# Ranking the weight split and the emptying of PSUM tiles sixty instructions earlier in a two-layer decoder trunk

## The chip, the cores and the metric

One core of one Trainium2 chip runs the whole kernel. The metric is the device time of one execution in microseconds (us); the time before is the median of three runs, 2280.33 us (2279.54 to 2280.35).

## The reference, cut to what matters

Two residual layers act on 256 tokens of width 2048, in float32. Each layer projects a normalised input to three groups of attention heads, mixes them back with `w_o`, and then runs a gated MLP with a short convolution:

```python
h = _rmsnorm(x, attn_norm[l])
z = jnp.einsum('bsd,de->bse', h, w_in[l])
...
x = x + jnp.einsum('bsm,md->bsd', mix, w_o[l])
h = _rmsnorm(x, ffn_norm[l])
u = jnp.einsum('bsd,df->bsf', h, w_up)          # 2048 -> 2 * 5632
u = conv(u) + conv_b                            # causal, 3 taps, per channel
a, g = jnp.split(u, 2, axis=-1)
x = x + jnp.einsum('bsf,fd->bsd', jax.nn.silu(g) * a, w_down)
```

All weights are float32, 410 MB in total, and each is used once.

## The kernel before, in words

**Weights.** The weights come as one stream of 128x128 blocks. `load` (L108) brings a chunk of 16 blocks (1 MB) into one of three `raw` tiles through the queue of SP. `convert` (L127) splits a piece of 8 blocks into two fp32r parts: ACT casts `raw` to `hi` (L139) and DVE subtracts to get `lo` (L140). There are five `hi` and five `lo` tiles, so a new piece can be cast only after TensorE (PE) has used up the piece five before it. `weights` (L145) hands a block out; at the first block of a piece it converts the piece two ahead (L150) and loads the next two chunks (L151, L152).

**Matmuls.** `mm_t` (L181) makes one 128-column output tile of all 256 tokens in a PSUM tile `mm`: 16 matmuls with `hi` against 512 columns (L193, both parts of the activations side by side) and 16 with `lo` against 256 columns (L198). It needs two pieces. Calls alternate: one does all of its `hi` first and then `lo`, the next does one `hi`, then `lo`, then the other fifteen `hi`. `mm_v` (L235) makes output tiles with tokens on the partitions (L247 to L249). `total` (L254) empties an `mm` tile of `mm_t`: ACT copies the second half out (L256), DVE adds the first half to it (L258).

**The MLP's up projection.** In each half of each layer, 22 pairs of tiles are made, an `a` tile and then a `g` tile. Of each tile, after `total`: GpSimd (POOL) multiplies by the norm's scale (L821), ACT applies a tap and the bias (L824), DVE adds two taps (L825, L826). After the second tile of a pair follow silu on ACT (L828), the product on POOL (L829), and the split of the result on ACT and DVE (L507, L508 in `to_hl`). After the 22 pairs, `residual` (L453) multiplies with `w_down` by `mm_v` and DVE adds the result to `x` (L458).

**What sets the order.** Every engine runs its instructions in the order in which they stand in its queue. That order is made by the framework's planner when the kernel is built. Each instruction has a rank, its place in the program. The planner keeps a clock of its own with an estimated duration for each instruction; whenever an engine is free on that clock, it gives it, among the instructions whose inputs are finished and whose tiles can be had, the one with the lowest rank. So an instruction that the program writes later often stands earlier in a queue, because it could run earlier on the planner's clock. On the chip the queue's order is then fixed, whatever the real durations are. `tc.high_priority(offset=60)` lowers the rank of the instructions in its block by 60, and these instructions do not advance the count of ranks. In one pair of the up projection the program has 90 instructions (64 matmuls, 8 of `convert`, 2 loads, 4 of `total`, 12 others).

Of the kernel before, what the change touches and what calls it, by code (L numbers as in the profile page):

```python
# [13 lines left out]
ALU = mybir.AluOpType  # L14
# [3 lines left out]
T = 256  # L18
# [8 lines left out]
MAGIC = 12582912.0  # L27
CH = 16
SUB = 8

C_ID, C_MASK, C_INVF, C_SIGN, C_EPS, C_SEL, C_ONE = 0, 128, 384, 386, 388, 390, 396
C_W = C_ONE + P
# [34 lines left out]
def kernel(ctx: ExitStack, tc: tile.TileContext, xin, xnat, pos, wstream, cst, par, fin, out):  # L67
    nc = tc.nc
# [10 lines left out]
    def nm(s):  # L79
        uid[0] += 1  # L80
        return f"{s}_{uid[0]}"
# [4 lines left out]
    def tmp():  # L86
        return work.tile([P, T], F32, tag="tmp", name=nm("tmp"), bufs=15)
# [10 lines left out]
    def f(ap):  # L98
        return ap.bitcast(F32)
# [4 lines left out]
    raws, subs = {}, {}  # L104
    bounds = [(c, i, min(SUB, n - i)) for c, (at, n) in enumerate(chunks) for i in range(0, n, SUB)]
    sub_of = {chunks[c][0] + o + i: (s, i) for s, (c, o, n) in enumerate(bounds) for i in range(n)}

    def load(c):  # L108
        if c >= nch or c in raws:
            return  # L110
        at, n = chunks[c]
        t = wpool.tile([P, CH * P], F32, tag="raw", name=nm("raw"), bufs=3)
        nc.sync.dma_start(t[:, : n * P], wflat[at * P * P : (at + n) * P * P].rearrange("(p e) -> p e", p=P))
        raws[c] = t
# [12 lines left out]
    def convert(s, between=None):  # L127
        if s >= len(bounds) or s in subs:
            return
        c, o, n = bounds[s]  # L130
        load(c)
        o = o * P
        src = raws[c][:, o : o + n * P]
        hi = wpool.tile([P, SUB * P], F32R, tag="hi", name=nm("hi"), bufs=5)
        lo = wpool.tile([P, SUB * P], F32R, tag="lo", name=nm("lo"), bufs=5)
        step = SUB // 2 * P if c < 3 else SUB * P
        for o in range(0, n * P, step):
            a = slice(o, min(o + step, n * P))
            nc.scalar.copy(hi[:, a], src[:, a])  # L139
            nc.vector.tensor_tensor(lo[:, a], src[:, a], f(hi[:, a]), ALU.subtract)  # L140
            if between is not None:
                between()
        subs[s] = (hi, lo)

    def weights(b, n=1):  # L145
        s, o = sub_of[b]
        if o == 0:
            convert(s)
            convert(s + 1)
            convert(s + 2)  # L150
            load(bounds[s][0] + 1)  # L151
            load(bounds[s][0] + 2)  # L152
        o *= P
        hi, lo = subs[s]
        return hi[:, o : o + n * P], lo[:, o : o + n * P]
# [25 lines left out]
    def mm_t(moving):  # L181
        ps = bank("mm", 3)
        k = len(moving)
        ws = []
        for i in range(k):
            ws.append(weights(cb[0]))
            cb[0] += 1
        flip = turn_of[0] % 2
        turn_of[0] += 1

        def high(part):
            for i in part:
                nc.tensor.matmul(ps, ws[i][0], moving[i], start=(i == 0), stop=bool(flip and i == k - 1))  # L193

        n = 1 if flip else k
        high(range(n))
        for i in range(k):
            nc.tensor.matmul(ps[:, :T], ws[i][1], moving[i][:, :T], start=False, stop=(not flip and i == k - 1))  # L198
        high(range(n, k))
        return ps  # L200

    def mm_first(moving, hooks={}, tag="mm", bufs=3):
        ps = bank(tag, bufs)
        k = len(moving)
        for i, mv in enumerate(moving):
            if i in hooks:
                hooks[i]()
            hi, lo = weights(cb[0])
            cb[0] += 1
            if i < k - 1:  # L210
                nc.tensor.matmul(ps, hi, mv, start=(i == 0), stop=False)
                nc.tensor.matmul(ps[:, :T], lo, mv[:, :T], start=False, stop=False)
            else:
                nc.tensor.matmul(ps[:, :T], lo, mv[:, :T], start=(i == 0), stop=False)
                nc.tensor.matmul(ps, hi, mv, start=False, stop=True)
        return ps

    def mm_t2(moving, hooks={}):
        ps = [bank("mm", 3) for _ in range(2)]
        k = len(moving)  # L220
        for i, mv in enumerate(moving):
            if i in hooks:
                hooks[i]()
            hi, lo = weights(cb[0], 2)
            cb[0] += 2
            for j in range(2):
                a = slice(j * P, (j + 1) * P)
                if i == 0:
                    nc.tensor.matmul(ps[j], hi[:, a], mv, start=True, stop=False)
                nc.tensor.matmul(ps[j][:, :T], lo[:, a], mv[:, :T], start=False, stop=False)  # L230
                if i:
                    nc.tensor.matmul(ps[j], hi[:, a], mv, start=False, stop=(i == k - 1))  # L232
        return ps
# [18 lines left out]
        return ps  # L252

    def total(ps, rows=P):  # L254
        t = tmp()
        nc.scalar.copy(t[:rows], ps[:rows, T : 2 * T])  # L256
        u = tmp()
        nc.vector.tensor_tensor(u[:rows], ps[:rows, :T], t[:rows], ALU.add)  # L258
        return u

    pr = [const.tile([P, Q_W], F32, tag=f"par{l}", name=f"par{l}") for l in range(DEPTH)]
# [301 lines left out]
    for l in range(DEPTH):  # L563
# [11 lines left out]
        else:  # L575
            first = mm_t2(hx, {4: lambda: norm.turn(3), KT // 2: norm.cols})
        rstd = norm.rows("rstd")
        u = total(first[0], 70)
        kf = tmp()
        nc.vector.tensor_tensor(kf[:70], u[:70], rstd[:70], ALU.mult)  # L580
# [23 lines left out]
        for i in range(8):  # L604
            a, b = scan[i % 2], scan[(i + 1) % 2]
            s = 1 << i
# [33 lines left out]
        for j in range(2):  # L640
            for h in range(H_FOX):
                if j == 0:
                    fqk.append(slot())
                i = j * H_FOX + h + 1
                u = total(first[i] if i < len(first) else mm_t(hx))
                nc.gpsimd.tensor_tensor(fqk[h][:, j * T : (j + 1) * T], u, rstd if j else rstd_f, ALU.mult)
                tick()
# [32 lines left out]
        for j in range(2):  # L680
            for h in range(H_DIFF):
                if j == 0:
                    aqk.append(slot())
                u = total(mm_t(hx))
                nc.gpsimd.tensor_tensor(aqk[h][:, j * T : (j + 1) * T], u, rstd if j else rstd_a, ALU.mult)
                if j == 1:
                    bg.append(rope_job(aqk[h][:], slot()[:], 0))
                tick()
# [43 lines left out]
        for qo in (Q_KN, Q_QN):  # L732
            ln = Norm(q_[:, qo : qo + 4], 512)
            tiles = []
            for k in range(4):
                u = total(mm_t(hx))
# [71 lines left out]
        for half in range(2):  # L808
            acts = []
            for i in range(HALF):  # L810
# [7 lines left out]
                for j in range(2):  # L818
                    u = total(pair[j] if pair else mm_t(hx))
# [181 lines left out]
```

## Time and profile before

| | |
|---|---|
| median of three runs | 2280.33 us |
| the profiled execution | 2280.38 us |
| its span, first to last instruction | 2278.2 us |
| busy: PE / DVE / ACT / POOL | 99% / 64% / 53% / 19% |
| granted PE clock, mean | 0.998 |
| DMA engines, mean busy share | about 0.5, 182 GB/s |

The profiled execution took 2.2 us more than its span, and agrees with the median to 0.05 us. The names of tiles in the rows are the program's: `hi`, `lo` and `raw` of the weights, `mm` for the PSUM tiles, `tmp` for the tiles of the steps after `total`.

### The profile page before, as it was taken

The numbers are of one execution on the slowest core, as the hardware profiler recorded it, in microseconds if no ns is written. First come the engines' busy times: TensorE is split into PE (matmuls) and PEld (weight loads), VectorE is DVE, ScalarE is ACT, GpSimd is POOL, SyncE is SP. The second block draws the span as 40 slices with busy tenths as digits, with TensorE's granted clock in tenths as the row PEclk, the third lists the DMA queues.
The fourth block names the chain that finished last, engine by engine and source line by source line (L and its number), as shares of the span: only waits on it lengthen the run. The fifth ranks groups of instructions, "written<-read, shape, count | busy, mean of one in ns | idle before, by whom it ended". The sixth has DMA issues, their size and how long they took to land.

```text
span 2278.2 us, 31040 instructions
## 1 busy us (share of the span) xinstructions
PE 2244.7 (99%) x12083; PEld 1931.5 (85%) x12083; DVE 1468.5 (64%) x2317; ACT 1198.6 (53%) x1867; POOL 436.6 (19%) x395
## 2 busy tenths in 40 slices
PE   9999999999999999999999999999999999999998
PEld 8888978888878888888888989788888888888886
DVE  8767766666664566665575677666666645777653
ACT  7456645555543455555454566456555434555543
POOL 4600000222210022220022001003333101222210
PEclk9999999999999999999999999999999999999999
DMA  8544344555555555545555444354555555555553
GB/s 314 203 149 167 142 149 176 173 179 169 182 197 191 185 178 173 184 168 204 189 181 201 150 165 153 138 183 178 185 185 186 208 197 185 187 191 193 205 198 116
DMA packets 60915, 413.59 MB, mean 182 GB/s; under 512 B 6880, under 2 KB 7008, under 8 KB 11744
## 3 DMA queue, kind: packets, MB, share of 16 engines
q1 hardware_dynamic: 60048, 410.54, 51.0%
q8 instruction: 95, 1.56, 0.3%
q10 hardware_dynamic: 720, 1.07, 0.1%
q14 instruction: 52, 0.43, 0.1%
HBM read 409.49 MB, written 2.10 MB: 181 GB/s over the span
## 4 chain that ended last, share of the span: by engine, by line
PE 84%; DVE 6%; ACT 5%; issue 3%; POOL 2%; DMA 0%; SPq 0%; ACTq 0%; POOLq 0%; DVEq 0%
PE mm L193 27%; PE mm L198 15%; PE mm L247 12%; PE mm L249 11%; PE mm L248 11%; DVE lo L140 4%; ACT hi L139 3%; PE s L470 2%; POOL tmp L821 2%; ACT tmp L824 1%; PE mm L232 1%; DVE tmp L825 1%; DVE tmp L826 1%; ACT tmp L828 1%; PE mm L763 1%
## 5 line engine op out<-in xcount | busy, mean ns | idle before, releaser
L140 DVE TENSOR_TENSOR lo<-raw,hi 128x1024 fp32r<-128x1024 f32 (+1 forms) x776 | 952.3, 1236 | 496.4 <-ACT hi L139 457.0
L139 ACT CAST hi<-raw 128x1024 fp32r<-128x1024 f32 (+1 forms) x776 | 799.3, 1039 | 469.1 <-PE mm L249 364.4
L193 PE MATMUL mm<-h,hi 128*128 128x512 f32 x3584 | 862.8, 392 | 0.0
L193 PEld LDWEIGHTS mm<-h,hi 128*128 128x128 f32 x3584 | 664.8, 188 | 134.5 <-ACT tmp L256 1.3
L198 PEld LDWEIGHTS mm<-h,lo 128*128 128x128 f32 x3584 | 462.0, 190 | 35.3 <-DVE lo L140 21.7
L198 PE MATMUL mm<-h,lo 128*128 128x256 f32 x3584 | 472.7, 284 | 15.8 <-DVE lo L140 15.8
L821 POOL TENSOR_TENSOR tmp<-tmp,rstd 128x256 f32<-128x256 f32 x176 | 224.3, 1274 | 1041.7 <-DVE tmp L258 731.7
L247 PE MATMUL mm<-hi,slot 128*128 128x512 f32 x992 | 388.8, 392 | 3.5 <-DVE tmp L258 3.5
L249 PE MATMUL mm<-hi,slot 128*128 128x512 f32 x992 | 385.5, 389 | 0.0
L248 PE MATMUL mm<-lo,slot 128*128 128x512 f32 x992 | 385.3, 388 | 0.0
L824 ACT ACTIVATE tmp<-tmp,par 128x256 f32<-128x256 f32 x176 | 105.9, 602 | 357.3 <-POOL tmp L821 357.1
L247 PEld LDWEIGHTS mm<-hi,slot 128*128 128x128 f32 x992 | 186.6, 188 | 46.1 <-DVE tmp L258 4.4
L249 PEld LDWEIGHTS mm<-hi,slot 128*128 128x128 f32 x992 | 186.6, 188 | 38.5
L248 PEld LDWEIGHTS mm<-lo,slot 128*128 128x128 f32 x992 | 186.8, 188 | 36.9
L825 DVE SCALAR_TENSOR_TENSOR tmp<-tmp,par,tmp 128x255 f32<-128x255 f32 x176 | 84.9, 482 | 204.0 <-ACT tmp L824 204.0
L829 POOL TENSOR_TENSOR tmp<-tmp,tmp 128x256 f32<-128x256 f32 x88 | 76.0, 863 | 208.8 <-ACT tmp L828 208.8
L256 ACT COPY tmp<-mm 128x256 f32<-128x256 f32 (+1 forms) x233 | 85.3, 366 | 56.5 <-PE mm L193 33.6
L258 DVE TENSOR_TENSOR tmp<-mm,tmp 128x256 f32<-128x256 f32 (+1 forms) x233 | 97.3, 417 | 4.3 <-ACT tmp L256 4.1
L826 DVE SCALAR_TENSOR_TENSOR tmp<-tmp,par,tmp 128x254 f32<-128x254 f32 x176 | 85.0, 483 | 6.2
L828 ACT ACTIVATE tmp<-tmp 128x256 f32<-128x256 f32 x88 | 36.8, 418 | 61.5 <-DVE tmp L826 61.4
L247 PE MATMUL mm<-hi,h 128*128 128x512 f32 (+1 forms) x192 | 68.3, 356 | 0.0
L249 PE MATMUL mm<-hi,h 128*128 128x512 f32 (+1 forms) x192 | 67.9, 354 | 0.0
(192 smaller groups left out, 1469.1 us busy)
## 6 DMA issues: line engine op xcount, KB each, us to landing
raw<-in_w SPq DMA_DIRECT2D x381, 1024.0 KB, 4.8
raw<-in_w SPq DMA_DIRECT2D x14, 256.0 KB, 5.4
slot<-in_x SPq DMA_DIRECT2D x8, 256.0 KB, 5.4
x<-in_xn SPq DMA_DIRECT2D x2, 1024.0 KB, 10.5
slot<-in_fin SPq DMA_DIRECT2D x4, 256.0 KB, 6.5
out<-x SPq DMA_DIRECT2D x4, 256.0 KB, 3.9
out<-x ACTq DMA_DIRECT2D x4, 256.0 KB, 4.2
par<-in_par SPq DMA_DIRECT2D x1, 325.0 KB, 7.5
```

The source lines that it names most:

```text
L139: nc.scalar.copy(hi[:, a], src[:, a])
L140: nc.vector.tensor_tensor(lo[:, a], src[:, a], f(hi[:, a]), ALU.subtract)
L193: nc.tensor.matmul(ps, ws[i][0], moving[i], start=(i == 0), stop=bool(flip and i == k - 1))
L198: nc.tensor.matmul(ps[:, :T], ws[i][1], moving[i][:, :T], start=False, stop=(not flip and i == k - 1))
L247: nc.tensor.matmul(ps[t][:, :n], s_hi, hi, start=(i == 0), stop=False)
L248: nc.tensor.matmul(ps[t][:, :n], s_hi, lo, start=False, stop=False)
L249: nc.tensor.matmul(ps[t][:, :n], s_lo, hi, start=False, stop=(i == k - 1))
L258: nc.vector.tensor_tensor(u[:rows], ps[:rows, :T], t[:rows], ALU.add)
L821: nc.gpsimd.tensor_tensor(uu, u, rstd, ALU.mult)
L824: nc.scalar.activation(y, uu, AF.Identity, scale=q_[:, w + 2 : w + 3], bias=q_[:, w + 3 : w + 4])
L825: nc.vector.scalar_tensor_tensor(y[:, 1:], uu[:, : T - 1], q_[:, w + 1 : w + 2], y[:, 1:], ALU.mult, ALU.add)
L826: nc.vector.scalar_tensor_tensor(y[:, 2:], uu[:, : T - 2], q_[:, w : w + 1], y[:, 2:], ALU.mult, ALU.add)
```

## The change

The conversion of the piece two ahead with the two loads behind it, and the two instructions of `total`, are put into blocks that lower their rank by 60. No instruction is added, removed or altered; only the order in which the planner takes them can change. The first two lines of `weights` stay as they were; but for the first pieces they do nothing, since the piece was converted two pieces earlier.

```diff
+AHEAD = 60
...
             convert(s)
             convert(s + 1)
-            convert(s + 2)
-            load(bounds[s][0] + 1)
-            load(bounds[s][0] + 2)
+            with tc.high_priority(offset=AHEAD):
+                convert(s + 2)
+                load(bounds[s][0] + 1)
+                load(bounds[s][0] + 2)
...
     def total(ps, rows=P):
-        t = tmp()
-        nc.scalar.copy(t[:rows], ps[:rows, T : 2 * T])
-        u = tmp()
-        nc.vector.tensor_tensor(u[:rows], ps[:rows, :T], t[:rows], ALU.add)
+        with tc.high_priority(offset=AHEAD):
+            t = tmp()
+            nc.scalar.copy(t[:rows], ps[:rows, T : 2 * T])
+            u = tmp()
+            nc.vector.tensor_tensor(u[:rows], ps[:rows, :T], t[:rows], ALU.add)
         return u
```

## Rows read from the trace of the kernel before

**Rows 1.** The page, busy time: engine, us, share of span, instructions

```profile
PE 2244.7 (99%) x12083; PEld 1931.5 (85%) x12083; DVE 1468.5 (64%) x2317; ACT 1198.6 (53%) x1867; POOL 436.6 (19%) x395
```

**Rows 2.** Waits of PE: us in total, times, longest us

```profile
PE mm L198 <- DVE lo L140: 15.8, 27, 0.6
PE mm L247 <- DVE tmp L258: 3.5, 2, 1.8
...
PE misc L358 <- DVE slot L546: 0.5, 1, 0.5
```

**Rows 3.** Busy time by stretch: length, then PE, PEld, DVE, ACT, POOL, clock, DMA

```profile
480.00:645.00 165.00, 156.77 (x886) 136.45 (x885) 105.22 (x153) 86.94 (x140) 43.08 (x41) 1.00 0.50 176
...
870.00:1030.00 160.00, 152.00 (x858) 131.99 (x856) 100.33 (x146) 83.88 (x136) 42.06 (x41) 1.00 0.50 177
1545.00:1770.00 225.00, 225.00 (x1296) 198.61 (x1295) 150.99 (x218) 128.24 (x201) 86.10 (x60) 1.00 0.52 185
```

**Rows 4.** Timeline of PE, first layer's up projection: start, us, what, idle before

```profile
567.64 1.23 PE L198 MATMUL mm<-h,lo 128*128 128x256 f32 x8 [0.60 <-DVE lo L140]
```

**Rows 5.** Timeline of PE, second half, where PE does not wait yet

```profile
841.89 7.25 PE L193 MATMUL mm<-h,hi 128*128 128x512 f32 x31
...
853.04 7.25 PE L193 MATMUL mm<-h,hi 128*128 128x512 f32 x31
```

**Rows 6.** Timeline of ACT over one pair of the first layer

```profile
564.97 0.42 ACT L828 ACTIVATE tmp<-tmp 128x256 f32<-128x256 f32 x1 [1.13 <-DVE tmp L826]
565.29 1.03 ACT L139 CAST hi<-raw 128x1024 fp32r<-128x1024 f32 x1
566.24 0.41 ACT L507 CAST slot<-tmp 128x256 fp32r<-128x256 f32 x1
566.55 0.36 ACT L256 COPY tmp<-mm 128x256 f32<-128x256 f32 x1
...
570.01 0.60 ACT L824 ACTIVATE tmp<-tmp,par 128x256 f32<-128x256 f32 x1 [2.16 <-POOL tmp L821]
570.52 1.99 ACT L139 CAST hi<-raw 128x1024 fp32r<-128x1024 f32 x2
...
578.51 0.36 ACT L256 COPY tmp<-mm 128x256 f32<-128x256 f32 x1
```

**Rows 7.** Timeline of DVE in the same pair

```profile
566.36 1.23 DVE L140 TENSOR_TENSOR lo<-raw,hi 128x1024 fp32r<-128x1024 f32 x1 [1.48 <-ACT hi L139]
567.50 0.42 DVE L508 TENSOR_TENSOR slot<-tmp,slot 128x256 fp32r<-128x256 f32 x1
567.84 0.41 DVE L258 TENSOR_TENSOR tmp<-mm,tmp 128x256 f32<-128x256 f32 x1
568.17 1.21 DVE L140 TENSOR_TENSOR lo<-raw,hi 128x1024 fp32r<-128x1024 f32 x1
```

**Rows 8.** Timeline of POOL in the same pair

```profile
568.33 1.65 POOL L821 TENSOR_TENSOR tmp<-tmp,rstd 128x256 f32<-128x256 f32 x1 [2.13 <-DVE tmp L258]
574.42 0.73 POOL L821 TENSOR_TENSOR tmp<-tmp,rstd 128x256 f32<-128x256 f32 x1 [4.45 <-DVE tmp L258]
```

**Rows 9.** Waits of ACT: us in total, times, longest us

```profile
ACT hi L139 <- PE mm L249: 364.4, 228, 2.4
```

**Rows 10.** Timeline of ACT, second layer's up projection, one pair

```profile
1601.05 0.37 ACT L256 COPY tmp<-mm 128x256 f32<-128x256 f32 x1
...
1612.34 0.37 ACT L256 COPY tmp<-mm 128x256 f32<-128x256 f32 x1
```

**Rows 11.** Timeline of DVE in the opening stage

```profile
21.81 3.49 DVE L546 TENSOR_TENSOR slot<-slot,slot 128x512 f32<-128x512 f32 x4
25.23 2.55 DVE L140 TENSOR_TENSOR lo<-raw,hi 128x1024 fp32r<-128x1024 f32 x2
```

**Rows 12.** Timeline of DVE at the end of a residual product

```profile
390.65 1.28 DVE L458 TENSOR_TENSOR x<-x,mm 128x512 f32<-128x512 f32 x2
```

**Rows 13.** Timeline of ACT at the same place

```profile
391.13 1.05 ACT L139 CAST hi<-raw 128x1024 fp32r<-128x1024 f32 x1 [1.65 <-PE mm L249]
```

## The prediction, made before the changed kernel was run

> **What bounds the kernel now.** I read the page's busy times first: PE is busy 99% of the span [rows 1], so only what PE loses by waiting can be won. The list of PE's waits comes second: nearly all of it is 27 waits of L198 for a `lo` of L140, none over 0.6 us, and two waits of L247 for L258 of 3.5 us together [rows 2]. Third, busy times by stretch say where: PE is idle 8.2 us of 165 and 8.0 us of 160 in the first layer's two up projections, and not at all in 225 us of the second layer's [rows 3]. So attention, the residual products and the second layer hold nothing to win.
>
> Fourth, one pair of the first layer, engine by engine. PE stops 0.60 us in the middle of an L198 group [rows 4]. The `lo` that it wants runs on DVE from 566.36 and had waited 1.48 us for ACT's cast [rows 7]; that cast stands on ACT behind the silu L828, for which ACT had been idle 1.13 us [rows 6]. ACT is not short of time; the queue's order keeps the cast behind an instruction whose input is late. From one L256 to the same one a pair later ACT needs 578.51 - 566.55 = 11.96 us [rows 6]. PE by itself needs 853.04 - 841.89 = 11.15 us [rows 5]. ACT's, DVE's and POOL's chain thus closes a ring longer by 0.81 us than PE's work; ACT falls behind by that much per pair, and once its lead is used up PE waits for it every time.
>
> What makes the ring long is one instruction on POOL: L821 takes 1.65 us at 568.33, and 0.73 us at 574.42 [rows 8]. The long one starts while DVE runs L140 from 568.17 to 569.38 [rows 7] and ends 0.60 us after it. Without those 0.92 us the ring would be 11.04 us, under PE's 11.15. The planner's order would be harmless had L821 taken 0.73 us each time. In the second layer the order differs; the ring is 1612.34 - 1601.05 = 11.29 us [rows 10], which over 21 pairs adds up to 3 us of lag and never reaches PE [rows 3].
>
> **The change part by part.** It alters ranks only. The planner takes, among instructions that can run on its clock, the lowest rank. So a rank matters only where two instructions of one engine are both ready when the engine comes free; elsewhere readiness decides.
>
> *The casts and L828, L824.* By the count of ranks, the cast behind L828 is written 40 counted instructions later (L828, L829, L507, L508, 32 matmuls, four steps of the next tile). Lowered by 60 it outranks L828 by about 20, and L824 of the same tile too. If both were ready together, the cast would move into ACT's 1.13 us of idle time, where its 1.03 us fit [rows 6], and the ring would be about 10.9 us. But were they? Between L824 and L828 of one tile lie L825 and L826 on DVE, so ACT must have been free there on the planner's clock as well, whatever its durations. A cast that could have run would have been taken then, at any rank. It was not, so its `hi` tile was not yet free by that clock, and a lower rank can't bring it ahead of L828. Likewise the two casts behind L824 at 570.01 [rows 6]: ahead of it come L258 and L821 on other engines, about 0.41 and 0.73 us [rows 7, 8], against one cast of 1.05 us that ACT has meanwhile, so ACT should have been free for a moment there too; this is less sure. On the chip these casts could have gone long before, since ACT runs late against PE; the planner's clock does not know of that. I take zero; the bounds are zero and all that can be won (below).
>
> *L256 and L258 of `total`.* L256 comes after L507 on ACT and L258 after L508 on DVE [rows 6, 7]. Here both may be ready: L508 and L258 both stand behind one L140. If they swap, L258 is 0.34 us earlier (567.50 instead of 567.84). It does not help L821 unless POOL gets in before the next L140: L508 then runs until 568.26 and the L140 behind it until 569.38 as before, and L821 ends 0.60 us after that, as now [rows 7, 8]. I take zero, with a bound of about -0.5 us per pair if POOL does get in, which is the second rival.
>
> The Trainium skill, "SBUF — State Buffer", section "SBUF: two separate sides", says that VectorE with two SBUF inputs and GpSimd take a shared port pair by turns, whichever starts first for its whole instruction. The 1.65 us against 0.73 us agree with that. By that rule POOL, which waits already, could get the pair when L508 ends, and the sum would be that of the second rival; no row shows two such DVE instructions back to back with POOL waiting from the first.
>
> *Casts elsewhere.* In `mm_v` stages ACT sits idle before the cast and waits for PE to use up the old `hi`: 228 times, 364.4 us [rows 9]. There the cast is already ahead of everything that it could overtake. Zero.
>
> *The loads.* They are the only work of SP's queue in the steady stages and keep their order among themselves; each is released by an L140. Zero. Cover: PE never waits for a load [rows 2]. If a load were late by its chunk, PE would show waits of L193 for L139.
>
> *The opening.* The pieces after the sixth are now ranked ahead of the last squares L546, whose sum PE needs at L358, where it waits 0.5 us already [rows 2]. The two L140 that stand behind L546 take 2.55 us [rows 11]. Bounds: 0 and +2.5 us. I take 0.5, near the lower end, since their `hi` tiles come free late there.
>
> *Background heads in attention.* Softmax steps may be overtaken by a cast of 1.05 us [rows 6] or an L140 of 1.22 us [rows 7]. PE shows no wait for them now [rows 2]; I allow -0.5 to +2 us and take zero.
>
> Sum: 2278.2 span + 2.2 outside it + 0.5 = 2280.9 us. The profiled execution agrees with the median (2280.38 and 2280.33), so no correction. Its own range is 2278 to 2285.
>
> **The rivals.** *First: the casts do come ahead of L828 or L824.* If my argument on the idle gap fails (the planner's estimates leave ACT busy there, or the order settles otherwise from the start), the first layer's rings fall under 11.15 us and all waits go. Price: 27 x 0.81 = 21.9 us, plus the two waits for L258 of 3.5 us: 2280.4 - 25.4 = 2255.0. For it: the rank distance (40) is inside 60. Against: the gap of 1.13 us that no cast used.
>
> *Second: L258 ahead of L508, and POOL gets in between.* L821 then ends at 568.26 + 0.60 = 568.86 instead of 569.98, the next L140 ends about 0.7 us later, and through the two casts and two L140 behind it L258 of the second tile comes some 0.5 us earlier. The ring is about 11.46 us, 0.31 over PE's; 21 pairs give 6.5 us of lag, about what ACT has in hand before PE waits today (nine pairs of 0.81 in the second half). Nearly all waits go: about 2257. For it: both behind one L140. Against: L508 may be ready, and done, before L258 on the planner's clock, and POOL must win the port.
>
> *Third, slower: an L140 overtakes L458.* After each column block of `residual` DVE empties two `mm` tiles, 1.28 us [rows 12], and PE needs one of them at once. An L140 taken first would add its 1.22 us [rows 7] to each of 32 blocks: +39 us, 2319; if at half of them, 2300. It decides whether a `lo` is ready when the block ends. Now the cast for it starts at 391.13, after 1.65 us of waiting for PE [rows 13], so its L140 can't start before 392.2, and L458 is done at 391.93. It is 0.3 us too late to overtake, and its rank is not what holds it. Unlikely.
>
> *Fourth: the change does nothing at all*, the queues being the same: 2280.4. It lies inside the forecast.
>
> **How the numbers follow.** No effect beyond the opening: 0.58, 2280.9 us, 2278 to 2285. First rival: 0.18, 2255. Second: 0.10, 2257. Slower (third rival, or heads in attention late): 0.14, of which half over 2290. The range 2254 to 2286 holds the forecast, both faster rivals and the mildest of the slower cases, less a little at either edge, some 0.85; without the faster ones it would leave out 0.28 at least. 0.2% (4.6 us) is what a measurement of this kernel can tell: faster 0.28, same 0.58, slower 0.14.
>
> **What would show it.** Right: the list of PE's waits still has 27 of L198 for L140; ACT's timeline in the first layer still reads L828, L139, L507, L256, and the ring 11.96 us. First rival: L139 stands between L824 and L828, the 27 waits are gone. Second: L258 before L508 and no L821 of 1.65 us in that place. Third: waits of L247 for L458. The opening: the wait of L358 for L546 grows. The forecast is wrong if the planner's clock leaves casts and other work ready together more often than the gaps suggest.

## The result, and the profile after

The changed kernel takes 2251.6 us (median; 2251.26 to 2251.88), the kernel before, run beside it, 2280.34 us (2279.54 to 2280.62). The ratio is 0.9874, with a 95% interval of 0.9857 to 0.9892: 1.3% faster. I had forecast no change (2280.9 us), with a range from 2254 to 2286: the time lies 2.4 us under its low end. The profiled execution's span is 2249.8 us against 2278.2.

In the code after, the lines have moved down by one to three: the cast L139 is L140, the subtract that makes `lo` L140 is L141, PE's L198 is L200, `total`'s copy L256 and add L258 are L259 and L261, the split L507 and L508 are L510 and L511, POOL's multiply L821 is L824, the silu L828 is L831, the opening's L358 is L361. Below, the lines of each kernel are its own.

PE's list of waits in the kernel after (us in total, times, longest), to be laid beside [rows 2]:

```profile
PE pv L274 <- DVE small L276: 1.5, 1, 1.5
PE misc L361 <- DVE slot L549: 0.8, 1, 0.8
PE mm L231 <- DVE h L397: 0.4, 1, 0.4
```

All 27 waits for a `lo` and both waits for L258 are gone. Busy times by stretch, in the columns of [rows 3], kernel after:

```profile
480.00:645.00 165.00, 165.00 (x942) 145.35 (x942) 120.80 (x166) 94.32 (x149) 34.45 (x45) 1.00 0.55 192
...
870.00:1030.00 160.00, 160.00 (x881) 139.57 (x880) 110.33 (x146) 87.88 (x133) 29.78 (x38) 1.00 0.54 191
```

PE fills both stretches, where it lacked 8.2 and 8.0 us. POOL is busy 34 and 30 us there instead of 43 and 42, which leads to the cause. DVE's timeline of one pair in the first layer, kernel after, beside [rows 7]:

```profile
568.09 1.23 DVE L141 TENSOR_TENSOR lo<-raw,hi 128x1024 fp32r<-128x1024 f32 x1 [1.49 <-ACT hi L140]
569.23 0.42 DVE L261 TENSOR_TENSOR tmp<-mm,tmp 128x256 f32<-128x256 f32 x1
569.57 0.42 DVE L511 TENSOR_TENSOR slot<-tmp,slot 128x256 fp32r<-128x256 f32 x1
569.90 1.77 DVE L141 TENSOR_TENSOR lo<-raw,hi 128x1024 fp32r<-128x1024 f32 x1
...
574.76 0.42 DVE L261 TENSOR_TENSOR tmp<-mm,tmp 128x256 f32<-128x256 f32 x1
...
580.31 0.42 DVE L261 TENSOR_TENSOR tmp<-mm,tmp 128x256 f32<-128x256 f32 x1
```

and POOL's, beside [rows 8]:

```profile
569.73 0.85 POOL L824 TENSOR_TENSOR tmp<-tmp,rstd 128x256 f32<-128x256 f32 x1 [1.73 <-DVE tmp L261]
...
575.26 0.74 POOL L824 TENSOR_TENSOR tmp<-tmp,rstd 128x256 f32<-128x256 f32 x1 [4.68 <-DVE tmp L261]
```

The add L261 now stands ahead of the split L511, where it stood behind it. POOL's multiply starts while L511 runs, ends at 570.58, which is 0.59 us after L511 ends (569.99), and takes 0.85 us instead of 1.65. The `lo` behind L511 pays for it: 1.77 us instead of 1.21. ACT's timeline, beside [rows 6]:

```profile
566.70 0.42 ACT L831 ACTIVATE tmp<-tmp 128x256 f32<-128x256 f32 x1 [1.13 <-DVE tmp L829]
567.02 1.04 ACT L140 CAST hi<-raw 128x1024 fp32r<-128x1024 f32 x1
568.03 0.41 ACT L510 CAST slot<-tmp 128x256 fp32r<-128x256 f32 x1
568.34 0.37 ACT L259 COPY tmp<-mm 128x256 f32<-128x256 f32 x1
...
579.41 0.37 ACT L259 COPY tmp<-mm 128x256 f32<-128x256 f32 x1
```

ACT's order is what it was, with the same 1.13 us of idle time ahead of the silu. But the ring closes in 579.41 - 568.34 = 11.07 us instead of 11.96. That is under PE's 11.15 us [rows 5], so ACT no longer falls behind. This is the second rival's mechanism, with its signs: L258 before L508, and no L821 of 1.65 us.

**Where the 28.4 us of span came from.** The same matmul stands 15.6 us earlier at about 660 us, and another 12.5 us earlier by about 1032; the rest of the kernel, second layer included, gains nothing. By terms: 27 waits at the 0.81 us per pair of the prediction give 21.9 us. The two waits for L258 cost more than their idle time, and the first of them was followed by a slow stretch. PE's timeline of the kernel before around both:

```profile
649.94 0.39 PE L249 MATMUL mm<-hi,slot 128*128 128x512 f32 x1
652.08 0.50 PE L247 MATMUL mm<-hi,slot 128*128 128x512 f32 x1 [1.75 <-DVE tmp L258]
652.42 0.40 PE L248 MATMUL mm<-lo,slot 128*128 128x512 f32 x1
...
654.99 0.63 PE L247 MATMUL mm<-hi,slot 128*128 128x512 f32 x1
655.42 0.63 PE L248 MATMUL mm<-lo,slot 128*128 128x512 f32 x1
...
1031.29 0.50 PE L247 MATMUL mm<-hi,slot 128*128 128x512 f32 x1 [1.76 <-DVE tmp L258]
```

At the first wait, 2.14 us pass from L249 to the L247 behind it, and 0.34 to the next matmul, where 0.23 each is usual: 2.0 us lost, and as much at the second wait, 4.0 for both. From 653.71 to 656.70 the starts lie 0.43 us apart instead of 0.23, which with the edges of that stretch is 1.6 us more. Together 21.9 + 4.0 + 1.6 = 27.5 us; 0.9 us I did not place.

### The profile page after: what moved, and what is told of

It is laid out like the page before. It is cut to its first block, busy times and chain, and to the rows that moved or that the text cites. A ratio compares the mean times of both kernels' runs of the same rounds, so it can differ in the third digit from the quotient of the medians.

```text
span 2249.8 us, 31033 instructions
## 1 busy us (share of the span) xinstructions
PE 2236.4 (99%) x12083; PEld 1929.6 (86%) x12083; DVE 1487.6 (66%) x2317; ACT 1204.2 (54%) x1867; POOL 404.7 (18%) x395
## 4 chain that ended last, share of the span: by engine, by line
PE 98%; ACT 1%; DVE 0%; DMA 0%; issue 0%; DVEq 0%; SPq 0%; ACTq 0%
PE mm L195 37%; PE mm L200 19%; PE mm L249 12%; PE mm L250 12%; PE mm L251 12%; PE s L473 2%; PE mm L234 1%; PE mm L766 1%; PE mm L767 1%; PE mm L768 1%; PE pv L505 1%; PE mm L232 1%; PE s L432 0%; PE misc L376 0%; PE pv L506 0%; ACT hi L140 0%
## 5 line engine op out<-in xcount | busy, mean ns | idle before, releaser
L141 DVE TENSOR_TENSOR lo<-raw,hi 128x1024 fp32r<-128x1024 f32 (+1 forms) x776 | 974.9, 1264 | 499.4 <-ACT hi L140 461.0
L140 ACT CAST hi<-raw 128x1024 fp32r<-128x1024 f32 (+1 forms) x776 | 800.5, 1039 | 475.7 <-PE mm L251 367.1
L200 PEld LDWEIGHTS mm<-h,lo 128*128 128x128 f32 x3584 | 460.6, 190 | 13.6
L200 PE MATMUL mm<-h,lo 128*128 128x256 f32 x3584 | 465.4, 283 | 0.0
L249 PE MATMUL mm<-hi,slot 128*128 128x512 f32 x992 | 387.7, 391 | 0.0
L824 POOL TENSOR_TENSOR tmp<-tmp,rstd 128x256 f32<-128x256 f32 x176 | 193.4, 1099 | 1037.7 <-DVE tmp L261 727.7
L249 PEld LDWEIGHTS mm<-hi,slot 128*128 128x128 f32 x992 | 186.3, 188 | 41.5 <-issue 4.0
L828 DVE SCALAR_TENSOR_TENSOR tmp<-tmp,par,tmp 128x255 f32<-128x255 f32 x176 | 84.5, 480 | 150.7 <-ACT tmp L827 150.7
L259 ACT COPY tmp<-mm 128x256 f32<-128x256 f32 (+1 forms) x233 | 85.9, 369 | 62.1 <-PE mm L195 34.1
L261 DVE TENSOR_TENSOR tmp<-mm,tmp 128x256 f32<-128x256 f32 (+1 forms) x233 | 97.4, 418 | 5.5 <-ACT tmp L259 5.3
L831 ACT ACTIVATE tmp<-tmp 128x256 f32<-128x256 f32 x88 | 36.8, 418 | 61.8 <-DVE tmp L829 61.7
L249 PE MATMUL mm<-hi,h 128*128 128x512 f32 (+1 forms) x192 | 68.3, 356 | 0.0
```

The lines of the kernel that those rows point to most:

```text
L249: nc.tensor.matmul(ps[t][:, :n], s_hi, hi, start=(i == 0), stop=False)
L824: nc.gpsimd.tensor_tensor(uu, u, rstd, ALU.mult)
```

## The experiments

Two theories stood at the start. A: the lift of `total` does it, by the swap of the add L258 and the split L508, which opens a gap ahead of the next `lo` in which POOL's multiply gets in. B: the lift of the weight split does it, the casts being taken earlier. Later runs take A apart: is it the add that is earlier, or POOL that is faster?

**One part alone: `total`.** Only the lift around `total`'s four lines:

```
     def total(ps, rows=P):
+        with tc.high_priority(offset=AHEAD):
             t = tmp()
...
```

> Only the two instructions of total are ranked 60 earlier; convert and its loads stay as before. Theory A (what helps is that the add L258 of the first tile of a pair goes ahead of the split L508 on DVE, so that POOL's L821 gets the port before the next lo): as fast as the change, 2250 to 2254 us, no wait of L198 for a lo. Theory B (the lifted casts do it): no gain, 2278 to 2283 us, the 27 waits of 0.6 us remain.

Measured: 2252.36 us (2252.07 to 2252.72), ratio 0.9881 [0.9866, 0.9896]; PE's list has no wait for a `lo`. This half alone is the whole gain, as far as the intervals tell.

**The other part alone: the weight split.**

```
             convert(s + 1)
+            with tc.high_priority(offset=AHEAD):
                 convert(s + 2)
                 load(bounds[s][0] + 1)
                 load(bounds[s][0] + 2)
```

> Only convert and its loads are ranked 60 earlier; total stays as before. Theory A: no gain, 2278 to 2283 us, the first layer's ring stays near 11.96 us. Theory B: 2250 to 2256 us. Since casts now outrank the copies and adds of total as well, a slower time (up to 2300 us) would say that total must keep pace with them.

Measured: 2321.19 us (2318.07 to 2322.71), ratio 1.0181 [1.0166, 1.0196], 42 us slower. Two views of this kernel: PE's waits, and ACT's timeline from the second tile of one pair to the next pair (the silu is L830 here, `total`'s copy L258 and add L260).

```profile
PE mm L200 <- DVE lo L141: 35.5, 54, 1.1
PE mm L249 <- DVE tmp L260: 13.9, 5, 5.1
```

```profile
570.53 1.04 ACT L140 CAST hi<-raw 128x1024 fp32r<-128x1024 f32 x1
571.76 0.42 ACT L830 ACTIVATE tmp<-tmp 128x256 f32<-128x256 f32 x1 [0.18 <-DVE tmp L828]
...
574.71 0.36 ACT L258 COPY tmp<-mm 128x256 f32<-128x256 f32 x1
...
587.10 0.37 ACT L258 COPY tmp<-mm 128x256 f32<-128x256 f32 x1
```

The ring is 12.39 us, longer than before, and the waits are twice as many and up to 1.1 us. The second layer, which lost nothing, loses 3.4 us in the stretch from 1545 to 1770 of [rows 3]. Casts and subtracts now outrank `total`: on ACT a cast of 1.05 us stands between the split and the copy of the next tile (from 573.76), on DVE a `lo` of 1.23 us ahead of the add (from 574.85), and the steps that lead to the next multiply come that much later. The cast also stands ahead of the silu here, and ACT's idle time ahead of the silu is 0.18 us instead of 1.13: this is the sign of the prediction's first rival. POOL's multiply takes 0.74 us for either tile (at 576.48 and 581.64). The ring is longer all the same. Theory B falls, and with it any idea that earlier casts are good in themselves. In the changed kernel both parts are lifted by the same sixty; ACT's order in a pair is that of the kernel before, and this harm does not come about.

**How far up: 30 and 40 in place of 60.** Counted as in the prediction, L258 stands 34 ranks behind L508 (32 matmuls and its own two steps), the cast 40 behind L828.

```
-AHEAD = 60
+AHEAD = 30
```

> The change with 30 in place of 60. By the count of ranks the add L258 of a tile is written 34 counted instructions after the split L508 of the pair before, so 30 is too little to bring it ahead and 35 or more is enough. Theory A: no gain, 2278 to 2283 us. Theory B has no step between 30 and 40 for the cast behind L828 (distance 40, so it needs more than 40): slow here as well as at 40.

Measured: 2279.86 us (2278.18 to 2282.02), ratio 1.0002 [0.9993, 1.0012]. PE's waits in this kernel are those of before, and POOL's multiply takes 1.65 us again, at 568.39:

```profile
PE mm L200 <- DVE lo L141: 15.9, 27, 0.6
```

```
-AHEAD = 60
+AHEAD = 40
```

> The change with 40 in place of 60. Theory A: 40 is over the distance of 34, so the full gain, 2250 to 2254 us. Theory B (casts ahead of L828, distance 40): still no gain, 2278 to 2283 us.

Measured: 2252.41 us (2252.25 to 2252.92), ratio 0.9881 [0.9864, 0.9897], with no wait for a `lo`. DVE's timelines say the same: with 30 the split starts at 567.55 and the add behind it at 567.89, with 40 the add at 568.53 and the split behind it at 568.87. The effect is a step between 30 and 40, where the distance of 34 lies, though the two runs would fit any other distance between them as well; from 40 to 60 nothing is added that the intervals can tell.

**One instruction: the DVE add.** The copy on ACT keeps its rank. The queues of PE, ACT and POOL are then the same as before; on DVE the add stands earlier.

```
         u = tmp()
-        nc.vector.tensor_tensor(u[:rows], ps[:rows, :T], t[:rows], ALU.add)
+        with tc.high_priority(offset=AHEAD):
+            nc.vector.tensor_tensor(u[:rows], ps[:rows, :T], t[:rows], ALU.add)
```

> The kernel before with one instruction ranked 60 earlier: the add L258 of total on DVE; the copy L256 on ACT, the casts and the loads stay. The queues of PE, ACT and POOL are those of the kernel before, on DVE the add and the split L508 change places in the MLP. Theory A (the order of these two on DVE alone): the full gain, 2250 to 2254 us. Theory C (the earlier copies and casts on ACT carry part of it): between, 2258 to 2280 us.

Measured: 2252.06 us (2251.72 to 2252.19), ratio 0.988 [0.9865, 0.9895]. POOL's multiply in this kernel:

```profile
568.35 0.85 POOL L823 TENSOR_TENSOR tmp<-tmp,rstd 128x256 f32<-128x256 f32 x1 [1.73 <-DVE tmp L260]
```

The whole gain hangs on the place of one 0.42 us instruction. It remains whether the add's being 0.34 us earlier counts, or what POOL makes of it. The next four runs ask that.

**More work on DVE, meant to open the gap.** The ranks are those of before; 88 additions of 0.42 us are put in, one behind the first tile of each pair, reading `total`'s result `u` and written to a tile that nothing uses.

```
...
+        if fill:
+            nc.vector.tensor_tensor(spill, ps[:, :T], u, ALU.add)
...
```

> The kernel before, all ranks as before, with 88 added adds of 128x256 on DVE, one behind the L258 of each pair's first tile in the MLP; it reads PSUM and one SBUF tile and its result is not used. It keeps the next lo off DVE for 0.42 us while POOL asks for its operands. Port theory (L821 takes 1.65 us only when a lo already runs): L821 falls to 0.74 us in that place, ring from 11.96 to about 11.4 us, most waits of PE go although work was added: 2252 to 2268 us. Rival (what counts is only that the add comes 0.34 us earlier, and DVE time is short): slower than before, 2283 to 2300 us, since each pair's ring gets 0.42 us longer.

Measured: 2286.12 us (2284.31 to 2288.45), ratio 1.0029 [1.0017, 1.004]. This missed: DVE's and POOL's timelines of this kernel show that the addition (L260) was placed behind the `lo`, not between it and the add.

```profile
568.49 0.42 DVE L258 TENSOR_TENSOR tmp<-mm,tmp 128x256 f32<-128x256 f32 x1
568.82 1.22 DVE L140 TENSOR_TENSOR lo<-raw,hi 128x1024 fp32r<-128x1024 f32 x1
569.96 0.42 DVE L260 TENSOR_TENSOR spill<-mm,tmp 128x256 f32<-128x256 f32 x1
```

```profile
568.99 1.65 POOL L824 TENSOR_TENSOR tmp<-tmp,rstd 128x256 f32<-128x256 f32 x1 [2.12 <-DVE tmp L258]
```

So it opened no gap, and tells the theories apart only in part: with POOL at 1.65 us the 27 waits stayed. The time lies in the range of the rival that the add must come earlier, but does not speak for it: the addition holds a PSUM tile longer, and PE waited 7.8 us for it at three places, where the kernel before has 3.5 us for L258.

**The multiply on DVE.** POOL's part is taken out of the question altogether.

```
-                    nc.gpsimd.tensor_tensor(uu, u, rstd, ALU.mult)
+                    nc.vector.tensor_tensor(uu, u, rstd, ALU.mult)
```

> The kernel before, all ranks as before, with the multiplication L821 on DVE in place of POOL (176 instructions, 0.42 us each there). Ring theory: with L821 no longer held up by a lo (1.65 us) and no hand-over to POOL, the first layer's ring is under PE's 11.15 us and the waits go: 2250 to 2256 us, unless the planner makes another order of DVE. Rival (the casts' place behind L828 is what holds PE up, whatever L821 takes): the 27 waits stay, 2276 to 2285 us.

Measured: 2251.74 us (2251.44 to 2252.3), ratio 0.9879 [0.9864, 0.9894], without any change of ranks. DVE's and ACT's timelines of this kernel:

```profile
567.03 0.42 DVE L258 TENSOR_TENSOR tmp<-mm,tmp 128x256 f32<-128x256 f32 x1
567.48 0.43 DVE L821 TENSOR_TENSOR tmp<-tmp,rstd 128x256 f32<-128x256 f32 x1
```

```profile
566.56 0.37 ACT L256 COPY tmp<-mm 128x256 f32<-128x256 f32 x1
...
574.46 1.05 ACT L139 CAST hi<-raw 128x1024 fp32r<-128x1024 f32 x1 [0.71 <-PE mm L193]
575.42 0.41 ACT L828 ACTIVATE tmp<-tmp 128x256 f32<-128x256 f32 x1
...
577.71 0.36 ACT L256 COPY tmp<-mm 128x256 f32<-128x256 f32 x1
```

The multiply takes 0.43 us and starts at once. The ring is 577.71 - 566.56 = 11.15 us, PE's own pace, because now the cast waits for PE. But the planner also made another order on ACT: the cast at 574.46 stands ahead of the silu L828, where it stood behind it [rows 6]. So the run shows a fast kernel with L258 still behind L508, but it does not separate the multiply that isn't held up from the cast's new place, which was the rival. The kernel after, the run with one add lifted and the next run do: there the cast stays behind the silu.

**The gap opened by useless work.** As two runs above, but the 88 additions read `t` in place of `u`, so that they can be taken before the `lo`. They stand directly behind the add; the other queues are those of before.

```
...
+        if fill:
+            nc.vector.tensor_tensor(spill, ps[:, :T], t, ALU.add)
...
```

> The kernel before, all ranks as before, with 88 added adds of 128x256 on DVE whose result is not used, as in the run with the filler, but reading the same two inputs as L258, so that in the queue each stands between the L258 of a pair's first tile and the next lo; the other queues are those of the kernel before. Port theory: POOL asks 0.5 us after L258 starts, finds no lo running, and L821 takes about 0.74 us in place of 1.65; the ring falls from 11.96 to about 11.5 us and most waits of PE go although DVE has 37 us more work: 2252 to 2270 us. Rival (the add must come earlier; DVE time is short): the lo comes 0.34 us later in each pair, 2280 to 2300 us.

Measured: 2255.3 us (2255.01 to 2255.69), ratio 0.9894 [0.9878, 0.9911]. PE's wait, then DVE's and POOL's timelines of this kernel:

```profile
PE mm L247 <- DVE spill L260: 2.0, 2, 1.6
```

```profile
565.72 0.42 DVE L258 TENSOR_TENSOR tmp<-mm,tmp 128x256 f32<-128x256 f32 x1
...
571.66 0.42 DVE L258 TENSOR_TENSOR tmp<-mm,tmp 128x256 f32<-128x256 f32 x1
571.99 0.41 DVE L260 TENSOR_TENSOR spill<-mm,tmp 128x256 f32<-128x256 f32 x1
572.33 1.65 DVE L140 TENSOR_TENSOR lo<-raw,hi 128x1024 fp32r<-128x1024 f32 x1
...
577.08 0.42 DVE L258 TENSOR_TENSOR tmp<-mm,tmp 128x256 f32<-128x256 f32 x1
```

```profile
572.15 0.74 POOL L824 TENSOR_TENSOR tmp<-tmp,rstd 128x256 f32<-128x256 f32 x1 [2.13 <-DVE tmp L258]
```

No wait for a `lo` is left in PE's list. The add stands no earlier in its queue than before; DVE has 88 x 0.42 = 37 us more to do; and the kernel is 24 us faster. POOL starts at 572.15, beside the addition (one input in PSUM, one in SBUF), is not held up by it, and ends at 572.89. The `lo` pays with 1.65 us. The ring, taken from add to add, is 577.08 - 565.72 = 11.36 us, above PE's 11.15 us, but 0.21 us a pair doesn't use up ACT's lead within the 22 pairs of a half.

**The add as early, but no gap.** As in the run with one add lifted, and the split L508 is held back until the next pair, so that a `lo` stands directly behind the add.

```
-                to_hl(a, ys[0])
+                nc.scalar.copy(a[:, :T], ys[0])
...
+                def split(a=a, src=ys[0]):
+                    nc.vector.tensor_tensor(a[:, T : 2 * T], src, f(a[:, :T]), ALU.subtract)
+
+                late.append(split)
...
+                    if late and j == 0:
+                        with tc.issue_after(tap.ins):
+                            late.pop()()
```

> As the run with one add ranked earlier, but the MLP's split L508 is held back until after L825 of the next pair, so that on DVE L258 stands ahead of it and the next lo directly behind L258; the queues of PE, ACT and POOL are those of the kernel before. L258 comes as early as in the fast kernels, or earlier. Port theory: the lo starts before POOL asks, L821 takes about 1.6 us again, the ring stays at 11.7 to 12.1 us: 2270 to 2288 us. Rival (the earlier add is what counts): as fast as with one add, 2250 to 2256 us.

Measured: 2274.45 us (2274.1 to 2274.74), ratio 0.9978 [0.9969, 0.9988]. PE's waits, DVE's and POOL's timelines of this kernel (the add is L260 here, the `lo` L141, the split L840, POOL's multiply L824):

```profile
PE mm L199 <- DVE lo L141: 13.1, 26, 0.5
```

```profile
566.28 0.42 DVE L260 TENSOR_TENSOR tmp<-mm,tmp 128x256 f32<-128x256 f32 x1
566.74 1.23 DVE L141 TENSOR_TENSOR lo<-raw,hi 128x1024 fp32r<-128x1024 f32 x1
...
569.63 0.42 DVE L840 TENSOR_TENSOR slot<-tmp,slot 128x256 fp32r<-128x256 f32 x1
...
572.63 0.42 DVE L260 TENSOR_TENSOR tmp<-mm,tmp 128x256 f32<-128x256 f32 x1
...
578.17 0.42 DVE L260 TENSOR_TENSOR tmp<-mm,tmp 128x256 f32<-128x256 f32 x1
```

```profile
566.78 1.78 POOL L824 TENSOR_TENSOR tmp<-tmp,rstd 128x256 f32<-128x256 f32 x1 [1.73 <-DVE tmp L260]
```

The add stands directly behind the earlier `lo`, as in the fast kernels, but POOL comes 0.04 us too late: it starts at 566.78, the `lo` at 566.74. (That `lo` had waited for its cast, which ends at 566.71 in ACT's timeline.) POOL ends 0.59 us after that `lo` (567.97) and takes 1.78 us. The ring is 578.17 - 566.28 = 11.89 us, and 26 waits remain. With the run before it this settles A: what counts is that POOL's multiply gets in ahead of the next `lo`. Where it does not, the earlier add does not bring the ring under PE's pace.

What the earlier add is worth by itself, in us of the kernel, this run does not show. From the second tile's add to the next pair's first the ring takes 578.17 - 572.63 = 5.54 us, where the kernel before took 5.94: that is the earlier add. From the first tile's add to the second's it takes 572.63 - 566.28 = 6.35 us instead of 6.02, and a part of that is the run's own: the split at 569.63 now stands ahead of the second tile's two `lo`. From the first tap (L825 of before) to the first of these `lo`, DVE's timeline has 1.13 us (569.23 to 570.36), against 0.94 before (570.65 to 571.59). My estimate of the ring without these 0.19 us is 11.70 us, still 0.55 over PE's 11.15.

## Why the prediction was wrong, step by step

*What bounds the kernel: right.* PE's waits in the first layer's up projections held nearly all that could be won, the ring of 11.96 us against 11.15 made them, and POOL's multiply of 1.65 us made the ring long. Where useless work let the multiply in (0.74 us) and the add stood no earlier, no wait for a `lo` was left. But the 11.04 us that I gave a ring without those 0.92 us was too short: the next `lo` pays for the multiply (1.65 us there), and the ring of that run is 11.36.

*The casts and L828, L824: zero was right, the reason is not borne out.* I took zero, from the 1.13 us of idle time that no cast had used. In the changed kernel the silu, cast, split and copy stand on ACT as before, the idle time too, and 40 ranks give what 60 give. The first rival did not happen, though its time, 2255, is near. A total near a rival's does not confirm the rival; the order on ACT, which I had named as its sign, does not show it. But I had argued that a lower rank can't bring the cast ahead of the silu, and in the run that lifts the weight split alone the cast does stand ahead of it (570.53 against 571.76). So the idle time did not show that the cast was not ready at any rank. Why it stays behind the silu when `total` is lifted too, no run shows. Nor did its new place bring the time that I gave the rival: that run took 42 us more, though casts overtake `total` in it as well.

*L256 and L258 of `total`: this step failed.* I took zero, "with a bound of about -0.5 us per pair if POOL does get in". Both conditions that the second rival needed were met. The add was ready when the split was on the planner's clock, since the swap came with an offset between 30 and 40, around the distance of 34. And POOL does get in between two DVE instructions that stand back to back. By the port rule that I cited there (the Trainium skill, "SBUF — State Buffer", section "SBUF: two separate sides"), the one of the two that starts first has the shared ports for its whole instruction, which allowed this outcome. The rows agree with its lock for a whole instruction: POOL's multiply ends 0.59 us after the DVE instruction ahead of it, be that a split of 0.42 us (after) or a `lo` of 1.23 us (last run), and the next `lo` grows from 1.21 to 1.77 us. I had no row against the rule in this place and gave it 0.10 all the same. For a case with a row for its mechanism [rows 7, 8] and a rule that allowed it, that was too little.

*The second rival's size: too small.* I put its ring at 11.46 us; it is 11.07. The half of a pair from the first tile's L258 to the second's shrank from 573.86 - 567.84 = 6.02 us to 574.76 - 569.23 = 5.53, by the 0.5 us that I had worked out. The other half, up to the next pair's first tile, shrank too, from 579.80 - 573.86 = 5.94 us to 580.31 - 574.76 = 5.55. I had left that out: the add stands 0.34 us earlier in the queue in every pair. The run with the gap opened, where the add stays in its place, has this half at 571.66 - 565.72 = 5.94 us as before. The starts of L258 in the pair of before that I use here are these (DVE, kernel before; its first, 567.84, is in [rows 7]):

```profile
573.86 0.42 DVE L258 TENSOR_TENSOR tmp<-mm,tmp 128x256 f32<-128x256 f32 x1
...
579.80 0.42 DVE L258 TENSOR_TENSOR tmp<-mm,tmp 128x256 f32<-128x256 f32 x1
```

The ring thus sank below PE's pace and no lag was left, where I had expected 6.5 us of lag in each half.

*The price of all waits: too small.* 27 x 0.81 held, but I priced the two waits for L258 by their idle time, 3.5 us. By the spacing of the matmuls they cost 4.0, and the stretch behind the first another 1.6. So the range's low end, 2254, which rested on that sum, was 2.4 us too high.

*The opening:* the wait at L358 grew from 0.5 to 0.8 us, where I took +0.5. It is 0.8 with the weight split lifted alone and 0.6 with `total` lifted alone, but the runs don't separate differences of that size.

*Attention, the loads, the residual products, the second layer: zero, as taken.* No wait of PE for a load or for L458 appeared, and 2319 (the third rival) is nowhere near. That 42 us could be lost by this kind of change was seen in the run that lifts the weight split alone, but by another way than I had named: casts and subtracts overtook `total`; L140 did not overtake L458.

## What to carry to other kernels

Where the bound engine waits a little and often, add up the ring of in-order queues that feeds it and compare it with the engine's own period: a ring 0.81 us too long cost 28 us here, and at 11.07 us, below the period of 11.15, none of the waits was left. Read which instruction in that ring is longer than its twin elsewhere, and what the neighbouring engine runs beside it; a short instruction that doesn't itself hold POOL up, even a useless one, placed between a producer on DVE and a long DVE instruction with two SBUF inputs can let a waiting POOL in. When a rank is lifted, lift also the steps that the lifted work would overtake and needs: the same casts cost nothing when `total` was lifted with them and 42 us when not.

## What the runs showed of the hardware

POOL's multiply, when a DVE instruction with two SBUF inputs holds it up, gets in before a second such instruction that stands directly behind: in the kernel after it ends 0.59 us after the split, and the `lo` behind the split takes 1.77 us instead of 1.21. An addition on DVE with one input in PSUM did not hold POOL up: 0.74 us beside it (571.99 to 572.40, in the run with the gap opened), as when undisturbed (0.73 in [rows 8]).

A short stop of PE can be followed by a stretch at the lower clock level, and need not be. Two windows of the kernel before (columns of [rows 3]), behind the two waits of 1.75 and 1.76 us:

```profile
654.00:657.00 3.00, 3.00 (x8) 2.28 (x8) 2.55 (x4) 2.53 (x4) 0.00 (x0) 0.52 0.45 186
...
1031.00:1034.00 3.00, 2.71 (x12) 2.25 (x13) 1.73 (x3) 1.00 (x2) 1.65 (x1) 1.00 0.79 257
```

Behind the first the granted clock was 0.52 in the mean of 3 us, the level of 1.2 GHz, with matmuls 0.43 us apart instead of 0.23; behind the second it stayed at 1.00, the level of 2.4 GHz. What decides between the two I did not try.
